# Attention: second score matmul over 128 rows instead of 64, rotary output split in place and stacked by copies

## The chip, the cores and the metric

One core of a Trainium2 chip runs the whole layer as one program. The metric is the device time of that program in microseconds (us); lower is better. The engines are TensorE (PE; its weight loads are shown apart as PEld), VectorE (DVE), ScalarE (ACT), GpSimd (POOL) and SyncE (SP), on whose queue all copies are issued here.

## What is computed

A decoder layer over 1024 tokens of width 1024: an mLSTM mixer and a differential attention in parallel, then cross attention, then a gated feed-forward part. The change lies in the differential attention, of 8 heads. Queries and keys of a head have two components `c` of 64 features, rotated by position; each component has its own causal softmax, and the second is subtracted with a factor:

```python
s = einsum('bhcqd,bhckd->bhcqk', qi, kt) * scale        # c = 0, 1; d = 64
s = where(kpos[None, :] <= qpos[:, None], s, -inf)
p = softmax(s, axis=-1)
a = p[:, :, 0] - lam * p[:, :, 1]
o = einsum('bhqk,bhkv->bhqv', a, vt)
```

Products are made nearly as exact as in float32: an operand is split into a high part (rounded to the type that PE takes fast, fp32r) and a low part, the rest; a product is the sum of high x high, high x low and low x high.

## The kernel before, in words

PE's order is written by hand. A queue of dense products (class `Weave`, L58) is issued in quanta, each of three or six matmuls, and the steps of the attention put their own matmuls between: `pump(n)` (L93) issues n quanta. The other engines' orders come from a list scheduler. All copies stand in one queue on SP, among them the loads of weights (`load_w`, L159), which the scheduler puts early.

For each head, `g_rope` (L606) makes queries (`which` 0) and keys (1): a dense product over 1024 features gives 128 rows, the two components of 64, by tokens, in two halves of 512 tokens. For each half, `ev` (L617) does: ACT reads the bank into `raw`; DVE shuffles it into `rot` and multiplies `raw` by a cosine; POOL multiplies `rot` by a sine; DVE adds. Then the result is split. Queries: tile `Q0` is to hold the high part of component 0 in rows 0 to 63 and its low part in rows 64 to 127, `Q1` the low part of component 1 above and its high part below. [...] Keys: `K0` holds the high part of component 0 twice, one above the other, `K1` that of component 1; a tile `klo` holds the low part of both components, 64 rows each.

So in `scores` (L664) one piece of scores takes two matmuls: L680 over 128 rows, (high + low of Q) x (high of K), and L681 over the 64 rows of one component, high of Q x low of K. In `Q1` and in `klo` component 1 lies in rows 64 to 127, so the second one uses rows 0 to 63 for component 0 and 64 to 127 for component 1. A block of 128 queries against n keys takes one or two such pieces per component; a head has 24, in groups `g` of two blocks, and after each piece one quantum of dense work. DVE reads each piece (L684, L687) for maximum and mask, ACT takes exp (L693), POOL scales the second component (L697), DVE combines (L698), and `values` (L702) transposes the weights on PE and multiplies by the values, a group later.

The buffers `raw`, `rot`, the values' `vt`, the gates' `gt` and the spills `ev` of the cross-attention products (L769) share a ring of `NROPE` buffers of 128x512. `Q`, `K` and `klo` have one buffer each, so the next head's halves wait for this head's last scores. Which dense products go into which head is set by `FILL` (L39); in head 7 these are products with 16 spills (`g_vo`) and the loads of the mLSTM's output (`g_load`).

Of the kernel before, what the change touches and what calls it, by code (L numbers as in the profile page):

```python
# [12 lines left out]
F = mybir.dt.float32  # L13
# [8 lines left out]
T = 1024  # L22
# [12 lines left out]
NROPE = 5  # L35
# [22 lines left out]
class Weave:  # L58
    """Order of the tensor engine's work: a queue of dense products, issued in quanta between
    the steps of the chains that wait for other engines, and steps that fall due after a  # L60
    number of quanta."""
# [54 lines left out]
def hybrid_layer(ctx: ExitStack, tc: tile.TileContext, a: dict, out: bass.AP):  # L116
# [74 lines left out]
    def g_fm(wsrc, acts, evac, pool=None, w=None):  # L191
        """128 features by the tokens of acts, K = 1024; evac(j, bank) per token half"""
# [10 lines left out]
    def g_tm(wsrc, nk, units, evac):  # L203
        """tokens by 256 features; units: (act pair, first token column); a bank holds two token tiles"""
# [41 lines left out]
    # ------------------------------------------- keys and values of the memory (cross attention)  # L246
# [42 lines left out]
    # ---------------------------------------------------------------- constants  # L289
# [42 lines left out]
    # ------------------------------------------------------------ mLSTM mixer  # L332
    with tc.tile_pool(name="ap", bufs=1, reuse_waits="tile") as A:
# [38 lines left out]
        def g_first():  # L372
            """values of head 0 and all input and forget gates: a bank per token tile"""
# [147 lines left out]
        # rotary tables  # L521
# [18 lines left out]
        # input and forget gates: partition = (head, chunk)  # L540
# [63 lines left out]
    # ------------------------------------------- differential attention mixer  # L604
    with tc.tile_pool(name="bp", bufs=1, reuse_waits="tile") as B:
        def g_rope(h, which):  # L606
            """rotary part of one head's queries or keys; stacked for two passes over 128 rows"""
            t_ = 16 + 8 * which + h
            if which == 0:
                dst = [B.tile([128, 1024], R, tag=f"Q{c}", name=f"Q{c}") for c in range(2)]  # L610
            else:
                dst = [B.tile([128, 1024], R, tag=f"K{c}", name=f"K{c}") for c in range(2)]
                klo = B.tile([128, 1024], R, tag="klo", name="klo")
                res["klo"] = klo
            res["Q" if which == 0 else "K"] = dst

            def ev(j, acc):  # L617
# [8 lines left out]
                to_hi(dst[0][:, js], raw, "g")  # L626
                to_hi(dst[1][:, js], raw, "s")
                if which == 0:
                    mv_ = B.tile([128, 512], R, tag="rhl", name="rlo", bufs=1)
                    to_lo(mv_, raw, dst[0][:, js], "v")  # L630
                    src = (mv_[0:64], mv_[64:128])
                else:
                    mv_ = B.tile([128, 512], R, tag="rhl", name="rhi", bufs=1)
                    to_hi(mv_, raw, "v")
                    to_lo(klo[:, js], raw, mv_, "v")
                    src = (mv_[0:64], mv_[64:128])
                dma(dst[0][64:128, js].bitcast(F), src[0].bitcast(F))
                dma(dst[1][0:64, js].bitcast(F), src[1].bitcast(F))
# [25 lines left out]
        def scores(h, g, qk):  # L664
            out_ = []
            for i in (2 * g, 2 * g + 1):
# [7 lines left out]
                for c in range(2):  # L674
                    run = None
                    for j, (c0, c1) in enumerate(cuts):
                        w = c1 - c0
                        sp = sm_tile("sp")
                        qs, cr = slice(i * 128, (i + 1) * 128), slice(c * 64, c * 64 + 64)
                        mm(sp[:, :w], qk[0][c][:, qs], qk[1][c][:, c0:c1], start=True)  # L680
                        mm(sp[:, :w], qk[0][c][cr, qs], qk[2][cr, c0:c1], stop=True)  # L681
# [91 lines left out]
        def g_qk(h):  # L773
            """Wq k^T of one head: [model dimension, memory keys]"""
# [12 lines left out]
        def g_vo(h):  # L787
            """v Wo of one head: [memory keys, model dimension]"""
# [175 lines left out]
    def pair(pool, tag, name, bufs):  # L964
        return (pool.tile([128, 8, 512], R, tag=tag, name=name + "h", bufs=bufs),
                pool.tile([128, 8, 512], R, tag=tag, name=name + "l", bufs=bufs))

    def g_add(wsrc, act, h, b, gb, dst=None):
        """z += act @ W for one half and 256 columns; the last block is followed by the norm"""
        def ev(u, acc):  # L970
            for i in range(2):
                ti = 4 * h + 2 * u + i
# [461 lines left out]
```

## Time and profile before

| what | us |
|---|---|
| median of three runs (lowest, highest) | 2325.5 (2322.64, 2325.77) |
| span of the profiled execution, first to last instruction | 2324.7 |
| PE busy in it | 2272.0 (98%), 14109 matmuls |
| DVE, ACT, POOL busy | 1437.7 (62%), 698.3 (30%), 730.1 (31%) |
| chain that ended last, share of PE | 85% |

Of the profiled execution no time but its span is shown; the median is 0.8 us above that span. The profile's page names the busy engine; what a stage waits for is read from the timeline of single engines (start, duration, instruction, and in brackets idle time before it with the releaser), and what a stretch holds from the table by windows. Starts of matmuls are measured; their ends are modelled, so durations of neighbours overlap.

### The profile page before, as it was taken

To read this page: it belongs to the slowest core of one execution; us is meant where nothing else is said; L and a number is where in the kernel's file an instruction comes from. 1 tells how busy PE (TensorE), PEld (TensorE's weight loads), DVE (VectorE), ACT (ScalarE), POOL (GpSimd) and SP (SyncE) were. 2 spreads that over 40 slices of the span, in tenths; PEclk is the share of its full clock that TensorE was granted. 3 is DMA by queue.
4 is the path that set the end of the run, shared out by engine and by line. 5 is a ranking of instruction groups with operands and counts; after the bars stand their busy time and mean duration, and the time that the engine had idled before them with its cause. 6 is when DMAs were issued, how large, how long until landed. Compare 5 with 4: busy or idle time off the path is not lost.

```text
span 2324.7 us, 36015 instructions
## 1 busy us (share of the span) xinstructions
PE 2272.0 (98%) x14109; PEld 2002.4 (86%) x14109; DVE 1437.7 (62%) x2671; ACT 698.3 (30%) x1375; POOL 730.1 (31%) x752
## 2 busy tenths in 40 slices
PE   8999999999999999999999999998899999999997
PEld 8898898877877877876888999998899999999996
DVE  8535644356677666667535477468866655566667
ACT  3322313234444444445332113313211111111122
POOL 7124413233243333334421223226411111211124
PEclk9999999999999999999999999999899999999999
DMA  8322212332142132126863423222211111111112
GB/s 315 113 62 86 100 46 100 121 108 71 42 135 77 42 109 65 49 68 196 278 214 136 175 89 101 82 91 64 64 47 46 55 55 55 46 46 55 55 57 98
DMA packets 87722, 221.68 MB, mean 95 GB/s; under 512 B 10080, under 2 KB 28416, under 8 KB 87552
## 3 DMA queue, kind: packets, MB, share of 16 engines
q1 hardware_dynamic: 87552, 219.37, 29.1%
q8 instruction: 111, 1.82, 0.3%
q14 instruction: 59, 0.48, 0.1%
HBM read 168.92 MB, written 41.98 MB: 91 GB/s over the span
## 4 chain that ended last, share of the span: by engine, by line
PE 85%; DVE 7%; POOL 2%; DMA 2%; issue 2%; ACT 1%; SPq 0%; DVEq 0%; POOLq 0%; ACTq 0%
PE acc L152 58%; PE xb L152 7%; PE xa L152 5%; PE xc L152 5%; PE sp L152 4%; PE op L152 2%; DVE wlo L149 1%; PE tp L727 1%; PE nm L152 1%; DVE d L1045 1%; DVE e L698 1%; PE kv L152 1%; ACT e L693 0%; DMA wraw<-oT_d 0%; DVE z L935 0%
## 5 line engine op out<-in xcount | busy, mean ns | idle before, releaser
L141 POOL TENSOR_SCALAR whi<-wraw 128x512 fp32r<-128x512 f32 (+1 forms) x250 | 181.7, 727 | 878.8 <-issue 355.4
L152 PE MATMUL acc<-bh,whi 128*128 128x512 f32 x1024 | 427.1, 417 | 0.9 <-DVE gt L849 0.5
L149 DVE TENSOR_TENSOR wlo<-wraw,whi 128x512 fp32r<-128x512 f32 (+1 forms) x379 | 307.6, 816 | 157.8 <-ACT whi L139 117.7
L152 PE MATMUL acc<-bh,wlo 128*128 128x512 f32 x1024 | 401.5, 392 | 0.0
L152 PE MATMUL acc<-bl,whi 128*128 128x512 f32 x1024 | 400.9, 392 | 0.0
L139 ACT ACTIVATE whi<-wraw 128x512 fp32r<-128x512 f32 (+1 forms) x252 | 157.6, 627 | 563.8 <-PE acc L152 284.2
L152 PEld LDWEIGHTS acc<-bh,whi 128*128 128x128 f32 x1024 | 192.8, 188 | 51.8 <-issue 15.7
L152 PEld LDWEIGHTS acc<-bh,wlo 128*128 128x128 f32 x1024 | 192.8, 188 | 42.1
L152 PEld LDWEIGHTS acc<-bl,whi 128*128 128x128 f32 x1024 | 193.3, 189 | 30.9
L152 PE MATMUL acc<-whi,bh 128*128 128x256 f32 (+1 forms) x728 | 218.5, 300 | 0.2 <-DVE ev L149 0.2
L152 PE MATMUL acc<-whi,bl 128*128 128x256 f32 (+1 forms) x728 | 205.5, 282 | 0.0
L152 PE MATMUL acc<-wlo,bh 128*128 128x256 f32 (+1 forms) x728 | 205.4, 282 | 0.0
L152 PE MATMUL xb<-xe,whi 128*128 128x256 f32 x1008 | 184.4, 283 | 11.0 <-DVE u L1045 8.1
L149 POOL TENSOR_TENSOR wlo<-wraw,whi 128x512 fp32r<-128x512 f32 (+1 forms) x125 | 174.0, 1392 | 9.8
L152 PEld LDWEIGHTS xb<-xe,whi 128*128 128x128 f32 x1008 | 156.4, 191 | 11.7 <-issue 7.2
L152 PEld LDWEIGHTS acc<-whi,bh 128*128 128x128 f32 x728 | 138.5, 190 | 11.2 <-issue 9.2
L152 PE MATMUL xb<-xe,wlo 128*128 128x256 f32 x504 | 143.0, 284 | 0.0
L152 PEld LDWEIGHTS acc<-wlo,bh 128*128 128x128 f32 x728 | 138.7, 191 | 0.8
L152 PEld LDWEIGHTS acc<-whi,bl 128*128 128x128 f32 x728 | 138.6, 190 | 0.0
L1255 DVE SCALAR_TENSOR_TENSOR z<-z,acc 128x512 f32<-128x512 f32 x144 | 98.2, 686 | 53.0 <-PE acc L152 51.6
L152 PE MATMUL xa<-xb,whi 128*128 128x256 f32 x672 | 125.1, 287 | 5.2 <-ACT u L1167 5.2
L152 PE MATMUL acc<-wlo,hidh 128*128 128x512 f32 x320 | 124.7, 390 | 1.4 <-DVE wlo L149 1.4
(320 smaller groups left out, 5257.9 us busy)
## 6 DMA issues: line engine op xcount, KB each, us to landing
wraw<-in_wfm_dram SPq DMA_DIRECT2D x48, 512.0 KB, 3.6
wraw<-in_wg_dram SPq DMA_DIRECT2D x24, 512.0 KB, 3.5
wraw<-in_wu_dram SPq DMA_DIRECT2D x24, 512.0 KB, 3.6
wraw<-in_wd_dram SPq DMA_DIRECT2D x22, 512.0 KB, 3.6
hT_d<-hp SPq DMA_DIRECT2D x16, 512.0 KB, 2.8
g_d<-gt SPq DMA_DIRECT2D x32, 256.0 KB, 2.2
gt<-g_d SPq DMA_DIRECT2D x16, 512.0 KB, 4.8
wraw<-in_wmix_dram SPq DMA_DIRECT2D x16, 512.0 KB, 4.2
```

Of the source, the lines that this page charges most:

```text
L139: S.activation(dst, src, AF.Copy)
L141: G.tensor_scalar(dst, src, 1.0, 0.0, op0=OP.mult, op1=OP.add)
L149: (V if eng == "v" else G).tensor_tensor(dst, src, hi.bitcast(F), op=OP.subtract)
L152: PE.matmul(o, l, r, start=start, stop=stop, skip_group_check=True)
L698: V.scalar_tensor_tensor(e[0][:, :n], e[0][:, :n], su[:, 0:1], e[1][:, :n], op0=OP.mult, op1=OP.add)
L727: PE.transpose(tp[:, kk * 256 + j * 128:kk * 256 + (j + 1) * 128], ab[j][:, kc], ident)
L1045: V.tensor_tensor(dst, x_, y_, op=op)
L1255: V.scalar_tensor_tensor(zs, zs, ALPHA if q == 0 else 1.0, acc, op0=OP.mult, op1=OP.add)
```

## The change

The high and the low part are now made in place: ACT writes the rounded high part of `raw` over `rot`, DVE the rest over `raw` (one subtraction). Everything else is done by copies of 64 rows x 512 tokens: four for a half of the queries (the high part of each component to its place, and the low part), eight for a half of the keys, of which the high part goes twice into `K0` or `K1` and the low part twice into `klo0` or `klo1`, one above the other. So the second matmul runs over 128 rows: (high + low of Q) x (low of K); the sum gains the term low x low. `klo` becomes two tiles, and the ring of shared buffers has four instead of five. The copies that POOL and ACT made of the high part, and DVE's copy `rhi`, are gone. Beside this the diff holds only comments and texts that were taken out.

```diff
@@ -35,1 +35,1 @@
-NROPE = 5
+NROPE = 4
@@ -601,18 +601,20 @@
                 W.pump(n)
         W.drain()
 
     with tc.tile_pool(name="bp", bufs=1, reuse_waits="tile") as B:
         def g_rope(h, which):
             t_ = 16 + 8 * which + h
+            dst = [B.tile([128, 1024], R, tag=f"{'QK'[which]}{c}", name=f"{'QK'[which]}{c}") for c in range(2)]
             if which == 0:
-                dst = [B.tile([128, 1024], R, tag=f"Q{c}", name=f"Q{c}") for c in range(2)]
+                res["Q"] = dst
+                to = [[(dst[0], 0), (dst[1], 64)], [(dst[0], 64), (dst[1], 0)]]
             else:
-                dst = [B.tile([128, 1024], R, tag=f"K{c}", name=f"K{c}") for c in range(2)]
-                klo = B.tile([128, 1024], R, tag="klo", name="klo")
-                res["klo"] = klo
-            res["Q" if which == 0 else "K"] = dst
+                klo = [B.tile([128, 1024], R, tag=f"klo{c}", name=f"klo{c}") for c in range(2)]
+                res["K"], res["klo"] = dst, klo
+                to = [[(kt, r) for kt in pr for r in (0, 64)] for pr in (dst, klo)]
 
             def ev(j, acc):
                 js = slice(j * 512, (j + 1) * 512)
@@ -623,19 +625,12 @@
                 V.tensor_tensor(raw, raw, cosT[:, js], op=OP.mult)
                 G.tensor_tensor(rot, rot, sinT[:, js], op=OP.mult)
                 V.tensor_tensor(raw, raw, rot, op=OP.add)
-                to_hi(dst[0][:, js], raw, "g")
-                to_hi(dst[1][:, js], raw, "s")
-                if which == 0:
-                    mv_ = B.tile([128, 512], R, tag="rhl", name="rlo", bufs=1)
-                    to_lo(mv_, raw, dst[0][:, js], "v")
-                    src = (mv_[0:64], mv_[64:128])
-                else:
-                    mv_ = B.tile([128, 512], R, tag="rhl", name="rhi", bufs=1)
-                    to_hi(mv_, raw, "v")
-                    to_lo(klo[:, js], raw, mv_, "v")
-                    src = (mv_[0:64], mv_[64:128])
-                dma(dst[0][64:128, js].bitcast(F), src[0].bitcast(F))
-                dma(dst[1][0:64, js].bitcast(F), src[1].bitcast(F))
+                to_hi(rot.bitcast(R), raw, "s")
+                V.tensor_tensor(raw.bitcast(R), raw, rot, op=OP.subtract)
+                for m, places in zip((rot, raw), to):
+                    for n, (t, r) in enumerate(places):
+                        c = n if which == 0 else n // 2
+                        dma(t[r:r + 64, js].bitcast(F), m[c * 64:c * 64 + 64])
             yield from g_fm(a["wfm"][t_], xT, ev)
 
         def g_vB(pr):
@@ -676,9 +671,9 @@
                     for j, (c0, c1) in enumerate(cuts):
                         w = c1 - c0
                         sp = sm_tile("sp")
-                        qs, cr = slice(i * 128, (i + 1) * 128), slice(c * 64, c * 64 + 64)
+                        qs = slice(i * 128, (i + 1) * 128)
                         mm(sp[:, :w], qk[0][c][:, qs], qk[1][c][:, c0:c1], start=True)
-                        mm(sp[:, :w], qk[0][c][cr, qs], qk[2][cr, c0:c1], stop=True)
+                        mm(sp[:, :w], qk[0][c][:, qs], qk[2][c][:, c0:c1], stop=True)
                         if j < len(cuts) - 1:
                             run = B.tile([128, 1], F, tag="run", name="run", bufs=2)
                             V.tensor_scalar(e[c][:, c0:c1], sp[:, :w], 1.0, None, op0=OP.mult, op1=OP.max,
```

What stands where is shown at three places. First PE, head 0, its first piece of scores for each component (`K_4362` and `K_4363` are K0 and K1 of that head): one piece of the difference.

```order
 L152 MATMUL acc<-bh,wlo 128x512
 L152 MATMUL sp<-K_4362,Q_4274 128x128
-L152 MATMUL sp<-klo,Q_4274 128x128
+L152 MATMUL sp<-klo_4364,Q_4274 128x128
 L152 MATMUL acc<-bh,whi 128x512
 L152 MATMUL acc<-bl,whi 128x512
 L152 MATMUL acc<-bh,wlo 128x512
 L152 MATMUL sp<-K_4363,Q_4275 128x128
-L152 MATMUL sp<-klo,Q_4275 128x128
+L152 MATMUL sp<-klo_4365,Q_4275 128x128
```

Only the tile of the second matmul differs, here and in all of PE's order; every matmul stands in the same place as before.

Second SP's queue where the keys of head 4 are made, of before (`rhi_7836` is the first half of 512 tokens, `rhi_7875` the second; `wraw` is a load of weights, `gt` a gate's spill):

```order
L638 DMA Q1_7604<-rlo_7777 64x512
L637 DMA K0_7781<-rhi_7836 64x512
L638 DMA K1_7782<-rhi_7836 64x512
L166 DMA wraw_8360<-in_wfm_dram 128x1024
L637 DMA K0_7781<-rhi_7875 64x512
L638 DMA K1_7782<-rhi_7875 64x512
L422 DMA g_d_76<-gt_7961 128x512
```

and with the change (`rot_7857` and `raw_7856` are the first half, `wraw_8395` is the same load of weights):

```order
L633 DMA Q1_7632<-raw_7796 64x512
L633 DMA K0_7809<-rot_7857 64x512 x2
L633 DMA K1_7810<-rot_7857 64x512 x2
L633 DMA klo0_7811<-raw_7856 64x512 x2
L633 DMA klo1_7812<-raw_7856 64x512 x2
L633 DMA K0_7809<-rot_7899 64x512 x2
L633 DMA K1_7810<-rot_7899 64x512 x2
L633 DMA klo0_7811<-raw_7898 64x512 x2
L633 DMA klo1_7812<-raw_7898 64x512 x2
L422 DMA g_d_76<-gt_7996 128x512
L166 DMA wraw_8395<-in_wfm_dram 128x1024
```

Eight copies stand where two stood, the low part's last, and the load of weights moves from between the halves to behind both and a spill.

Third POOL at the same place, before (`rot_7828` is the keys' first half):

```order
L754 TENSOR_TENSOR of_7760<-of_7760,rt_7807 128x256
L624 TENSOR_TENSOR rot_7828<-rot_7828,sinT_815 128x512
L141 TENSOR_SCALAR K0_7781<-raw_7827 128x512
L141 TENSOR_SCALAR whi_8051<-wraw_8045 128x512
L624 TENSOR_TENSOR rot_7867<-rot_7867,sinT_815 128x512
L141 TENSOR_SCALAR K0_7781<-raw_7866 128x512
L697 TENSOR_SCALAR e1_7904<-e1_7904,ssum_7906 128x128
```

and with the change:

```order
L749 TENSOR_TENSOR of_7788<-of_7788,rt_7836 128x256
L626 TENSOR_TENSOR rot_7857<-rot_7857,sinT_815 128x512
L141 TENSOR_SCALAR whi_8086<-wraw_8080 128x512
L626 TENSOR_TENSOR rot_7899<-rot_7899,sinT_815 128x512
L692 TENSOR_SCALAR e1_7939<-e1_7939,ssum_7941 128x128
```

POOL's copies of the high part are gone, the rest stands as before.

## Rows read from the trace of the kernel before

**Rows 1.** Table by windows: stretch, length, busy us (instructions) of each engine, clock, DMA share, GB/s.
```profile
497.60:1120.40 622.80, 613.10 (x3172) 474.33 (x3172) 424.36 (x1032) 279.34 (x598) 228.54 (x250) 0.99 0.31 94
```

**Rows 2.** Timeline of PE, head 1: start us, us, engine, line, instruction.
```profile
600.84 0.34 PE L152 MATMUL sp<-K,Q 128*128 128x384 f32 x1
601.11 0.43 PE L152 MATMUL sp<-klo,Q 64*128 64x384 f32 x1
601.48 0.39 PE L152 MATMUL acc<-whi,bh 128*128 128x256 f32 x1
601.70 0.28 PE L152 MATMUL acc<-wlo,bh 128*128 128x256 f32 x1
601.82 0.28 PE L152 MATMUL acc<-whi,bl 128*128 128x256 f32 x1
```

**Rows 3.** Timeline of PE's weight loads, same place; in brackets idle time before.
```profile
601.11 0.18 PEld L152 LDWEIGHTS sp<-klo,Q 64*128 64x128 f32 x1 [0.19 <-issue]
601.47 0.19 PEld L152 LDWEIGHTS acc<-whi,bh 128*128 128x128 f32 x1 [0.18 <-issue]
```

**Rows 4.** View of the tile klo: count, duration ns min/median/max, first and last start, forms.
```profile
L152 PE MATMUL sp<-klo,Q x192: 323/438/502, 497.8 to 1112.4; 64*128 64x384 f32 x80, 64*128 64x512 f32 x64, 64*128 64x256 f32 x32, 64*128 64x128 f32 x16
```

**Rows 5.** View of the tile raw, same columns: copies that the change takes out.
```profile
L143 DVE CAST rhi<-raw x16: 426/426/561, 483.0 to 1065.5; 128x512 fp32r<-128x512 f32 x16
L141 POOL TENSOR_SCALAR K<-raw x16: 622/852/862, 483.1 to 1065.6; 128x512 fp32r<-128x512 f32 x16
```

**Rows 6.** Timeline of SP, head 4: copies of the first half of the keys.
```profile
818.68 0.46 SPq L637 DMA_DIRECT2D K<-rhi  x1
819.25 0.54 SPq L638 DMA_DIRECT2D K<-rhi  x1
```

**Rows 7.** DMA issues from 497 to 1064: count, KB each, median us to landing.
```profile
K<-rhi SPq DMA_DIRECT2D x26, 128.0 KB, 2.2
```

**Rows 8.** Timeline of DVE: cast of the keys' first half, heads 2, 4, 5, 6.
```profile
652.50 0.43 DVE L143 CAST rhi<-raw 128x512 fp32r<-128x512 f32 x1
...
817.75 0.43 DVE L143 CAST rhi<-raw 128x512 fp32r<-128x512 f32 x1
...
896.96 0.43 DVE L143 CAST rhi<-raw 128x512 fp32r<-128x512 f32 x1
...
984.28 0.56 DVE L143 CAST rhi<-raw 128x512 fp32r<-128x512 f32 x1 [0.43 <-DMA Q<-rlo]
```

**Rows 9.** Timeline of PE: first klo matmul of heads 2, 4, 5, 6.
```profile
657.63 0.33 PE L152 MATMUL sp<-klo,Q 64*128 64x128 f32 x1
...
821.76 0.33 PE L152 MATMUL sp<-klo,Q 64*128 64x128 f32 x1
...
901.25 0.33 PE L152 MATMUL sp<-klo,Q 64*128 64x128 f32 x1
...
987.89 0.33 PE L152 MATMUL sp<-klo,Q 64*128 64x128 f32 x1
```

**Rows 10.** Windows: sum over 16 stretches, 8 pieces each, groups 2 and 3.
```profile
sum 178.60, PE 178.60 PEld 118.69 DVE 114.23 ACT 75.18 POOL 45.16; mean PE 11.16 PEld 7.42 DVE 7.14 ACT 4.70 POOL 2.82
```

**Rows 11.** Waits in the attention stage: us in total, times, longest us.
```profile
PE tp L727 <- DVE e L698: 8.6, 6, 2.2
...
DVE e L687 <- PE sp L152: 46.4, 64, 1.9
```

**Rows 12.** Windows: head 7, from its first score to the first product after.
```profile
1064.00:1120.40 56.40, 55.37 (x236) 37.86 (x235) 39.40 (x104) 33.40 (x72) 26.44 (x29) 1.00 0.92 294
```

**Rows 13.** DMA issues in head 7.
```profile
vo_d<-ev SPq DMA_DIRECT2D x14, 256.0 KB, 8.0
```

**Rows 14.** Windows: a stretch after PE's wait for softmax in head 0.
```profile
559.20:562.60 3.40, 3.40 (x12) 2.73 (x11) 2.57 (x6) 1.33 (x3) 0.62 (x1) 0.50 0.30 69
```

**Rows 15.** Timeline of SP, head 4: a load of weights.
```profile
820.84 0.33 SPq L166 DMA_DIRECT2D wraw<-in_wfm_dram  x1
```

**Rows 16.** Timeline of PE: the first product that uses these weights.
```profile
867.07 0.50 PE L152 MATMUL acc<-bh,whi 128*128 128x512 f32 x1
```

## The prediction

> **What bounds the kernel now.** I read the page first, to see which engine is busy nearly all the time and whose work makes up the chain that ended last: both are TensorE (PE). Then the table by windows, for the stage that the change touches, from the first score matmul at 497.6 us to the first product after the attention at 1120.4 us: 622.80 us, of which PE is busy 613.10, DVE 424.36, ACT 279.34 and POOL 228.54 [rows 1]. So time on PE is time. But a busy PE is not PE at its peak, so the next view is PE's timeline, where the reader is to look at the distance between *starts*, not at the durations. One dense 256-column product starts 0.12 us after another (601.70, 601.82). The pair that makes a piece of scores is slower: the 128-row matmul of K starts at 600.84, the 64-row matmul of klo at 601.11, the next dense product at 601.48 and the one after at 601.70 [rows 2]. That is 0.86 us from 600.84 to 601.70, for columns (384 + 384 + 256) that at 0.12 us per 256 would take 0.18 + 0.18 + 0.12 = 0.48 us. So **0.38 us** are lost at each pair: some 0.09 after the 128-row matmul, 0.19 after the 64-row one, 0.10 after the dense one behind it. PE's weight-load timeline says how: the load for the 64-row matmul begins only when that matmul itself begins, after 0.19 us in which the loader stood idle for nothing that the profile names, and the 128-row load after it again waits 0.18 us [rows 3]. Between matmuls that are all 128 rows high the loads lie under the matmul before, and the idle time is gone. There are 192 such pairs, in widths from 128 to 512 columns [rows 4].
>
> **The change part by part.**
>
> *Second score matmul over 128 rows.* The order of PE is the same row for row; only klo's height changes. If the cost hangs on the change of height, each pair loses its 0.38 us: 192 x 0.38 = **-73 us**, all on the path, since PE is what waits. I take the 384-column row for all widths (80 of the 192 have it); the 16 narrowest pairs may give less, as their weight loads set their pace. The matmul itself has the same columns, so the extra 64 rows cost nothing in this pace. A rule speaks against this term: the Trainium skill, "TensorE: Matmul & The Clock Gate", Part 3 (What overlaps and what doesn't), says that a weight load overlaps a running matmul only where the two use different row groups. By that rule the 128-row load of klo would wait as the 64-row one does, the term would be about 0 and the sum would come out as in the rival on height below. The rows disagree: loads of 0.19 us at matmuls that follow each other every 0.12 us, all on the same 128 rows [rows 2, 3], must overlap.
>
> *Copies on the engines.* POOL loses 16 copies of keys of 0.85 us and as many of queries, 27 us at most, DVE 16 casts of 0.43 us (7 us) [rows 5]; ACT's count stays. None of them is PE time, and POOL is busy for 37% of the stage. I cost it at nothing; if it helps, it is in the low end.
>
> *More DMA and a later arrival of keys.* A half (512 tokens) of a head's queries goes from two copies to four, of its keys from two to eight: over 8 heads of two halves, 64 become 192 issues on SP, each of 0.46 to 0.54 us and 0.57 us apart [rows 6], landing 2.2 us after issue [rows 7]. What can be late is the first half of the keys at a head's start. Now DVE's cast of K starts at 817.75 in head 4 [rows 8] and its first klo matmul at 821.76 [rows 9]. After the change the hi part is cast by ACT in about that place, 0.65 us; the first copy starts 0.5 us later (cast ends 818.18, copy starts 818.68 [rows 6, 8]), so 1.13 us after the point where the cast starts now. The first score needs both copies of klo0, the fifth and sixth in the queue: start 1.13 + 5 x 0.57 = 3.98, landing 2.2, so 6.2 us after that point. Head 4: 823.95 against 821.76, a wait of 2.2 us. The same for the other heads whose keys come late: head 2, 652.50 + 6.2 against 657.63, 1.1 us; head 5, 896.96 against 901.25, 1.9 us; head 6, 984.28 against 987.89, 2.5 us, less 0.4, since there the cast waited for a copy of the buffer that the change takes out [rows 8, 9]. Together **+7 us**. The second score, of the other component, comes after a dense step and waits for copies 2 x 0.57 us later; I cost it at nothing. Lower end 0 (POOL, freed of its copies, finishes the rotation sooner); upper end 16, where each landing takes twice the 2.2 us and four heads pay 2.2 us more.
>
> *Softmax behind a faster PE.* In the 16 stretches where eight pairs stand together (the scores of 512 to 1024 keys) DVE is busy 114.23 of 178.60 us [rows 10]. With 16 x 8 x 0.38 = 49 us less it would be 88% busy, on the path of exp, POOL's scaling and the transposes. PE now waits for that chain six times, 8.6 us in all [rows 11]. It is not overrun on average, but a piece of scores may be late. Bounds: 0, and one piece of 1.02 us (178.60 / 128 - 0.38) in each of the 16 stretches, 16 us; nearer the first, since it is DVE that now waits for scores (64 times, 46.4 us [rows 11]) and that has time to lose: **+5 us**.
>
> *Head 7.* From 1064 to 1120.4 the DMA engines are 92% busy at 294 GB/s [rows 12], and spills land after 8.0 us [rows 13]. The change cuts the buffers that spills, gates and rotary halves share from five to four. The 16 spills there need 4 rounds of some 8.5 us, 34 us, about the time that would be left for them. Head 7's share of the gain is 24 x 0.38 = 9.1 us; between none and all of it is lost: **+6 us**, nearer all than none because DMA has so little room.
>
> *Clock.* After one of the waits for softmax the granted clock was 0.50 for 3.4 us [rows 14], the lower of its two levels (1.2 GHz), which costs half of that, 1.7 us. Longer waits may bring one more such stretch: **+2 us**; bounds 0 and eight of them, 14 us.
>
> Sum: -73 + 7 + 5 + 6 + 2 = -53. The profiled span is 2324.7 us, so 2271.7; no time is shown for what lies around this span, and the median of the runs is 0.8 above it. I say **2272 us**.
>
> **The rivals.**
>
> *All of it is hidden.* POOL's 27 us make the rotation earlier, the chain keeps up, and the whole 73 us come through: 2252. For it: PE waits only 8.6 us in the stage now [rows 11]. Against: head 4's keys have no slack, and head 7's DMA none.
>
> *The chains become the pace.* All upper ends together would give -73 + 16 + 16 + 9 + 14 = -18, 2307; halfway from my sum to there, -35, stands for this case: 2290. For it: DVE at 88% [rows 10]. Against: DVE's 46.4 us of waiting for scores [rows 11].
>
> *Height is not the cause.* The loss belongs to the pair, whatever its rows: PE keeps its pace, the keys still come late, 2324.7 + 7 = 2332. By the rule of the Trainium skill above (same page and section) this is the case. Against: the dense products are 128 rows high, add into one bank as well, and keep 0.12 us [rows 2].
>
> *Weights come late (slower).* Weight loads stand in the same SP queue. In head 4 one is issued at 820.84, between the two halves of the keys, and used at 867.07 [rows 15, 16]; in the new order it stands behind the second half's eight copies and a gate's spill. If loads came 8 us too late in each of eight heads, PE would lose 64 us more: 2336. The point from which this makes the kernel slower is 53 / 8 = 6.6 us of waiting per head. Against: the margin there is 46 us, and the added issues of a head are 16 x 0.57 = 9 us.
>
> **How the numbers follow.** The forecast 0.65, all hidden 0.17, chains as the pace 0.12, height not the cause 0.03, weights late 0.03. The first three are all faster than by 0.2% (4.7 us, about what a measurement of this kernel can tell from no change); of the last two's 0.06 I give 0.02 to no change, for mixtures. Faster 0.94, same 0.02, slower 0.04. The range goes from just above the all-hidden case to the chain case: 2254 to 2294; the bounds of keys (0 to 16) and of head 7 lie inside it.
>
> **What would show it.** On PE's timeline the pair's two starts and the next one should be 0.17 to 0.18 us apart for 384 columns, with no idle time of the weight loader; the stage from first score to the first product after should take about 570 us. At heads 2, 4, 5 and 6 the first score should wait 1 to 2 us for a copy of klo. POOL and DVE lose 32 and 16 instructions. I am wrong if the 64-row gaps stay in the pairs, if ACT or SP are found waiting for the four shared buffers in every head, or if the transposes wait for DVE by more than some 15 us in all.

## The result, and the profile after

| | before | after |
|---|---|---|
| median, us (lowest to highest of 4 runs each) | 2324.18 (2322.64 to 2325.77) | 2286.71 (2285.06 to 2288.24) |
| span of the profiled execution, us | 2324.7 | 2283.3 |

The ratio is 0.9837, with a 95% interval of 0.9823 to 0.9851: faster, by 37.5 us of the medians and 41.4 us of the two profiled spans. The forecast was 2272, 53 us below the time before; the measured time lies in its range, 15 us above the forecast.

The page's first line shows what left the engines: no matmul, 32 instructions of POOL (720 for 752) and 16 of DVE (2655 for 2671).

```profile
PE 2207.3 (97%) x14109; PEld 2008.0 (88%) x14109; DVE 1421.2 (62%) x2655; ACT 696.4 (30%) x1375; POOL 704.9 (31%) x720
```

PE's timeline of the kernel after (start, duration, instruction; in brackets idle time before it and its releaser) at a pair of 384 columns in head 1, at the start of head 2, and in head 7:

```profile
600.42 0.34 PE L152 MATMUL sp<-K,Q 128*128 128x384 f32 x1
600.60 0.34 PE L152 MATMUL sp<-klo,Q 128*128 128x384 f32 x1
600.77 0.29 PE L152 MATMUL acc<-whi,bh 128*128 128x256 f32 x1
600.90 0.28 PE L152 MATMUL acc<-wlo,bh 128*128 128x256 f32 x1
...
641.30 0.22 PE L152 MATMUL sp<-K,Q 128*128 128x128 f32 x1
643.30 0.30 PE L152 MATMUL sp<-klo,Q 128*128 128x128 f32 x1 [1.77 <-DMA klo<-raw]
...
1061.67 0.40 PE L152 MATMUL sp<-klo,Q 128*128 128x512 f32 x1
1068.43 0.79 PE L152 MATMUL acc<-whi,kvh 128*128 128x512 f32 x1 [6.37 <-ACT ev L765]
```

The first four rows answer to [rows 2]: starts 0.18, 0.17 and 0.13 us apart, 0.48 in all where it was 0.86. The weight loader's (PEld's) timeline at the same pair answers to [rows 3]; there is no idle time in it, and the load for the 128-row klo begins at 600.43, while the matmul of K, on the same 128 rows, runs from 600.42:

```profile
600.30 0.19 PEld L152 LDWEIGHTS sp<-K,Q 128*128 128x128 f32 x1
600.43 0.19 PEld L152 LDWEIGHTS sp<-klo,Q 128*128 128x128 f32 x1
600.60 0.19 PEld L152 LDWEIGHTS acc<-whi,bh 128*128 128x128 f32 x1
```

The other four rows of PE's timeline are new: a wait for a copy of klo at a head's start, and one of 6.4 us in head 7. PE's waits over the attention (what waited, for what; us in total, times, longest) answer to [rows 11], where the transposes' 8.6 us for `e` stood:

```profile
PE tp L722 <- DVE e L693: 12.7, 7, 3.6
PE sp L152 <- DMA klo<-raw: 9.0, 7, 2.3
PE acc L152 <- ACT ev L765: 6.4, 1, 6.4
PE op L152 <- DVE atl L149: 3.7, 7, 1.6
PE acc L152 <- ACT whi L139: 1.0, 1, 1.0
```

The table by windows (window, its length, busy time and instructions of PE, PEld, DVE, ACT and POOL, granted clock, DMA share, GB/s) has the whole stage, from the first score to the mark at which [rows 1] end; then the seven stretches at half the clock, against [rows 14]; then five microseconds of head 7, against [rows 12]; last, of the kernel before, the only other stretch at half clock in its stage:

```profile
497.80:1082.20 584.40, 551.42 (x3172) 482.14 (x3171) 411.11 (x1018) 278.22 (x600) 205.71 (x222) 0.98 0.44 128
...
551.50:554.90 3.40, 2.71 (x8) 2.33 (x9) 3.12 (x5) 1.12 (x2) 0.90 (x1) 0.51 0.02 5
643.70:647.10 3.40, 3.40 (x18) 3.40 (x17) 3.29 (x9) 1.79 (x4) 1.41 (x1) 0.50 0.52 130
698.30:701.70 3.40, 3.08 (x9) 2.57 (x10) 3.09 (x6) 1.12 (x2) 0.53 (x1) 0.50 0.00 0
797.30:800.70 3.40, 3.07 (x9) 2.62 (x10) 1.14 (x7) 0.88 (x4) 0.00 (x0) 0.50 0.88 205
872.40:875.80 3.40, 3.40 (x10) 2.82 (x11) 1.60 (x10) 0.88 (x4) 0.23 (x1) 0.50 0.70 164
954.30:957.70 3.40, 3.40 (x11) 2.82 (x11) 1.14 (x7) 0.88 (x4) 0.37 (x1) 0.50 0.88 204
1066.90:1073.70 6.80, 5.27 (x12) 4.12 (x13) 1.96 (x4) 2.99 (x5) 0.62 (x1) 0.50 1.06 379
...
1060.00:1065.00 5.00, 2.06 (x11) 1.44 (x9) 2.16 (x9) 3.05 (x6) 2.71 (x4) 1.00 1.04 396
...
719.70:723.10 3.40, 3.40 (x13) 2.82 (x12) 1.95 (x4) 0.94 (x2) 0.14 (x1) 0.51 0.27 63
```

The stage is 584.4 us where it was 622.8, so 38.4 of the 41.4 us came from it. (The mark at its end is not the end of the attention: the last product of the values starts at 1135.3 before and at 1097.2 after. These are 38.1 us apart, so the reading stands.) The rows add up, nearly. *Pairs:* from the matmul of K to the second instruction behind it, 176 pairs take 0.38 to 0.40 us less, the 16 of 128 columns 0.28 (0.46 for 0.74): -73. *Waits:* 9.0 for klo, 12.7 + 3.7 - 8.6 = 7.8 for the softmax and its split, 6.4 + 1.0 = 7.4 in head 7: +24. *Clock:* PE was busy in 24.3 of 27.2 us at half clock, which costs, as an estimate, half of that, 12.2; in the kernel before, in all 6.8 us of two such stretches, 3.4 (the other is [rows 14]): +9. Together -40, against the measured -38.4. All seven stretches begin behind, or in, one of the eight waits of PE of more than 1.7 us; the eighth (2.64 us, for `e`, up to 1006.29) has none behind it. Five of the eight are new, the four for klo at heads 2, 4, 5 and 6 and the one for `ev`, and each of these five has a stretch. In the kernel before, two of three waits of 2.1 to 2.2 us have one.

Where the 6.4 us in head 7 come from is read on ACT's timeline: three spills stand still until one of the four buffers has been written out, while the DMA share is 1.04 to 1.06:

```profile
1067.78 1.86 ACT L765 ACTIVATE ev<-acc 128x512 f32<-128x512 f32 x3 [3.83 <-DMA vo_d<-ev]
```

### The profile page after: what moved, and what is told of

Its sections match the earlier page's. It is cut to its first block, busy times and chain, and to the rows that moved or that the text cites. A ratio compares the mean times of both kernels' runs of the same rounds, so it can differ in the third digit from the quotient of the medians.

```text
span 2283.3 us, 36224 instructions
## 1 busy us (share of the span) xinstructions
PE 2207.3 (97%) x14109; PEld 2008.0 (88%) x14109; DVE 1421.2 (62%) x2655; ACT 696.4 (30%) x1375; POOL 704.9 (31%) x720
## 4 chain that ended last, share of the span: by engine, by line
PE 51%; DVE 5%; DMA 2%; issue 2%; POOL 1%; ACT 1%; SPq 0%; DVEq 0%; POOLq 0%; ACTq 0%
PE acc L152 32%; PE xb L152 7%; PE xa L152 5%; PE xc L152 5%; DVE wlo L149 1%; DMA vo_d<-ev 1%; PE sp L152 1%; DVE d L1040 1%; PE op L152 1%; DVE z L930 0%; DVE xb L149 0%; PE tp L722 0%; DVE z L926 0%; DVE u L1040 0%; PE tp L1007 0%
## 5 line engine op out<-in xcount | busy, mean ns | idle before, releaser
L152 PE MATMUL acc<-bh,whi 128*128 128x512 f32 x1024 | 418.1, 408 | 0.4 <-ACT gtok L389 0.4
L152 PE MATMUL acc<-whi,bh 128*128 128x256 f32 (+1 forms) x728 | 213.2, 293 | 0.2 <-DVE ev L149 0.2
```

What stands on the lines that cost most here:

```text
L152: PE.matmul(o, l, r, start=start, stop=stop, skip_group_check=True)
```

## The experiments

Medians are of each kernel's runs; the kernel before was run beside each batch (medians 2324.36 to 2325.66), and the ratios are to that. A quantum is one step of the queue of dense products in `Weave`; filling work is what these quanta put between the steps of the attention; a seam is the place where one head ends and the next begins.

Where a few us decide, the end of the kernel is a poor place to look: behind the attention all these kernels have the same matmuls, and yet their profiled executions take 1152 to 1157 us there, with 21 to 34 us at half clock. So the time from the first score to one and the same place behind the attention (with 7850 matmuls left) is given as well, from the profiled execution: 671.7 us in the kernel before, 633.4 in the changed one.

**One line back.** The second matmul over 64 rows again, all else as changed:

```diff
-                        mm(sp[:, :w], qk[0][c][:, qs], qk[2][c][:, c0:c1], stop=True)
+                        mm(sp[:, :w], qk[0][c][cr, qs], qk[2][c][cr, c0:c1], stop=True)
```

> The changed kernel with one line back: the second score matmul runs over the 64 rows that hold the high part of the queries, as before the change; rotary output, copies and buffers stay as changed. Theory A (the change of height costs about 0.39 us in each of 192 pairs, and it alone is the gain): the pairs stand 0.86 us apart again in place of 0.47 (384 and 256 columns), +74 us, of which some 20 to 30 us are hidden again because the slower pace lets the key copies and the softmax catch up: 2330 to 2345 us, thus slower than the kernel before (2324). Theory B (the gain comes from fewer POOL and DVE instructions or from the copies, the height is incidental): 2283 to 2292 us, as the changed kernel, with pairs still 0.47 us apart.

Measured 2346.12 us (2337.70 to 2348.95), ratio 1.009 [1.0069, 1.0111]. PE's timeline of it, the pair that answers to [rows 2]:

```profile
600.24 0.34 PE L152 MATMUL sp<-K,Q 128*128 128x384 f32 x1
600.51 0.43 PE L152 MATMUL sp<-klo,Q 64*128 64x384 f32 x1
600.87 0.39 PE L152 MATMUL acc<-whi,bh 128*128 128x256 f32 x1
601.09 0.28 PE L152 MATMUL acc<-wlo,bh 128*128 128x256 f32 x1
```

The distance of 0.85 us is back, and each other width has its own of before. So the height is the gain, 59 us of it at the end of the kernel, and the rest of the change is a loss: without its matmul the kernel is 22 us slower than before. The profile is of the fastest execution, 13 us slower than before, and its waits account for that: PE waits 22.6 us in the stage where it waited 9.5, 8.0 of them for klo and 6.4 for `ev`, neither of which the kernel before has, and 10.2 us are at half clock for 6.8. The other three executions are 8 to 11 us longer, with a mean granted clock of 0.986 to 0.989 where this one has 0.993; no profile shows where. Theory A stands a little beyond its own upper end.

**The ring of shared buffers alone, on the kernel before** (`NROPE = 5` to `4`).

> The kernel before with the shared ring of rotary, value and spill buffers cut from 5 to 4, and nothing else. Theory A (the ring costs only in head 7, where the spills of v Wo wait for their copies out, and the slower pairs of the kernel before hide most of it): 2324 to 2330 us. Theory B (the smaller ring costs in every head, since the rotary output waits for the spills): 2330 to 2345 us. Theory C (head 7's wait in the changed kernel is due to full DMA queues, whatever the ring): 2322 to 2325 us.

Measured 2330.91 us (2325.67 to 2331.64), ratio 1.0028 [1.0015, 1.0040]: 6.6 us, at the edge of A and B. Its profile, taken in an execution of 2327.39 us, has 3.1 us of PE's waits for `ev`, both in head 7, a stretch of 6.8 us at half clock there, and no new wait in the other heads. Up to the same place it takes 4.1 us more than the kernel before. The ring costs in head 7, a few us, also with the slow pairs; what the longer executions have more is not shown.

**Order turned round in every second pair, on the kernel before.**

```diff
+                        odd = (c * len(cuts) + j) % 2 == 1
+                        if odd:
+                            mm(sp[:, :w], qk[0][c][cr, qs], qk[2][cr, c0:c1], start=True)
-                        mm(sp[:, :w], qk[0][c][:, qs], qk[1][c][:, c0:c1], start=True)
-                        mm(sp[:, :w], qk[0][c][cr, qs], qk[2][cr, c0:c1], stop=True)
+                        mm(sp[:, :w], qk[0][c][:, qs], qk[1][c][:, c0:c1], start=not odd, stop=odd)
+                        if not odd:
+                            mm(sp[:, :w], qk[0][c][cr, qs], qk[2][cr, c0:c1], stop=True)
```

> The kernel before, but every second pair issues its matmul of 64 rows first, so that two matmuls of 64 rows stand together and two of 128 rows stand together: 96 round trips between heights in place of 192, the same 192 matmuls of 64 rows. Theory A (the cost is in the change of height, 0.39 us a round trip): -37 us less what waits give back, 2287 to 2297 us. Theory B (the cost is in each matmul of 64 rows, or in each of its weight loads): 2322 to 2326 us. Theory C (also a step from rows 0 to 63 to rows 64 to 127 costs as much): where one chunk a tile is scored the two short matmuls are of different halves, 32 of the 96 saved round trips would stay: -25 us, 2299 to 2304 us.

Measured 2324.77 us, ratio 1.000 [0.9990, 1.0009], what B foresaw. But its timeline shows that the experiment did not do what its text says:

```profile
600.88 0.28 PE L152 MATMUL acc<-whi,bl 128*128 128x256 f32 x1
601.09 0.44 PE L152 MATMUL sp<-klo,Q 64*128 64x384 f32 x1
601.46 0.44 PE L152 MATMUL sp<-K,Q 128*128 128x384 f32 x1
601.74 0.28 PE L152 MATMUL acc<-whi,bh 128*128 128x256 f32 x1
```

Dense products stand between any two pairs, so each 64-row matmul still has 128-row ones on both sides, and the number of round trips is unchanged. It tells nothing between A and B. What it does show is that the cost hangs on place and not on operand: 0.21 into the short matmul, 0.37 out of it, 0.28 from the 384-column matmul behind it, which takes 0.18 among its like, the same sum as in [rows 2] though K and klo have changed places.

**Two pairs at a time, short matmuls next to each other, on the kernel before.**

```diff
+                    for sp, (c, (c0, c1)) in zip(sps, pairs):
+                        mm(sp[:, :c1 - c0], qk[0][c][:, qs], qk[1][c][:, c0:c1], start=True)
+                    for sp, (c, (c0, c1)) in zip(sps, pairs):
+                        cr = slice(c * 64, c * 64 + 64)
+                        mm(sp[:, :c1 - c0], qk[0][c][cr, qs], qk[2][cr, c0:c1], stop=True)
...
+                        yield 2 * PUMP_S
```

> The kernel before, but the scores are issued two pairs at a time: two matmuls of 128 rows, then two of 64 rows next to each other, then twice the filling products. The matmuls are the same 192 of 64 rows, the round trips between the heights fall from 192 to 96 (the run with the order turned round in every second pair left them at 192, since filling products of 128 rows stand between any two pairs). Theory A (the cost is in the change of height, 0.39 us a round trip): -37 us, of which waits may give back some 10: 2287 to 2300 us. Theory B (the cost is in each matmul of 64 rows or its weight load): 2322 to 2328 us. Theory C (a step from rows 0 to 63 to rows 64 to 127 costs as much as one from 128 to 64): 32 of the 96 are not saved, -25 us, 2299 to 2304 us.

Measured 2298.37 us (2298.12 to 2299.06), ratio 0.9887 [0.9872, 0.9902], 26 us faster with the same 192 matmuls of 64 rows. B is out. The number lies in A's range and only 0.6 us outside C's; the rows decide. First a block with two short matmuls of different halves (rows 0 to 63, then 64 to 127), then one with two of the same half, both of 512 columns:

```profile
503.21 0.61 PE L152 MATMUL sp<-K,Q 128*128 128x512 f32 x2
503.76 0.50 PE L152 MATMUL sp<-klo,Q 64*128 64x512 f32 x2
504.19 0.50 PE L152 MATMUL acc<-bh,whi 128*128 128x512 f32 x1
...
533.91 0.63 PE L152 MATMUL sp<-K,Q 128*128 128x512 f32 x2
534.47 0.73 PE L152 MATMUL sp<-klo,Q 64*128 64x512 f32 x2
535.13 0.50 PE L152 MATMUL acc<-bh,whi 128*128 128x512 f32 x1
```

From the first short matmul to the next dense product it is 0.66 us for two of the same half and 0.43 for two of different halves; one alone takes 0.42 to 0.43 in the kernel before. So a second one of the same half costs its columns (0.23) and nothing for a change; and one of the other half costs nothing at all (in all 32 such blocks its start is 3 to 4 ns behind that of the first). C has it the wrong way round. By these rows the edit saves 96 x 0.38 = 36 us and 32 second matmuls of 0.06 to 0.23, 5 us more; 13 us of new waits (22.4 for 9.5 us in PE's waits, 15.1 of them for `e`) leave 28, and 26 were measured. The Trainium skill, "TensorEngine Tiling (Array Packing)", Key Properties, says that changing the tiling mode drains TensorE, and that different tiles can work at the same time. Both agree with these rows: 0.38 us for going to 64 rows and back, and two halves in the time of one.

**Low part of the keys written in place beside rows of zeros.** No copies of klo; DVE writes 64 rows of each tile, the other 64 stay zero, and the second matmul keeps its 128 rows.

```diff
-                to = [[(kt, r) for kt in pr for r in (0, 64)] for pr in (dst, klo)]
+                to = [[(kt, r) for kt in dst for r in (0, 64)]]
...
+                    for c in range(2):
+                        cr = slice(c * 64, c * 64 + 64)
+                        V.tensor_tensor(res["klo"][c][cr, js], raw[cr], rot[cr], op=OP.subtract)
```

> The changed kernel, but the low part of the keys is not copied: it is written by two DVE subtractions of 64 rows each into two fixed tiles whose other 64 rows are zero throughout, so the second matmul still runs over 128 rows; the product of the two low parts is left out of the scores as in the kernel before. It has 64 copies fewer on SP's queue and 16 DVE subtractions more. Theory A (the late copies of the low part at heads 2, 4, 5 and 6 give back 9 us, and the half-clock stretches behind these four waits about 1.7 us each): 2269 to 2278 us, no wait for a copy at these heads, and at most 3 half-clock stretches in the stage in place of 7. Theory B (the copies' wait only stands in for a wait on DVE's softmax, which is the pace): 2282 to 2288 us, with the lost time at waits on e. Theory C (half-clock stretches come with the faster pace itself and not with the waits): 2276 to 2280 us, with 6 or 7 stretches left.

Measured 2282.57 us (2280.67 to 2285.20), ratio 0.9823 [0.9808, 0.9838]: 4.1 us below the changed kernel, in B's range. PE's waits in the stage:

```profile
PE tp L730 <- DVE e L701: 16.8, 11, 3.3
PE op L152 <- DVE atl L149: 6.9, 10, 1.6
PE acc L152 <- ACT ev L773: 3.0, 2, 2.4
```

The 9.0 us for klo are gone, as A said, and 3.4 of those for `ev`, but 7.3 are back at DVE's results (16.8 + 6.9 for 12.7 + 3.7), and six half-clock stretches are left where A allowed three. Six is what C foresaw, but each of them stands behind, or in, a wait of 1.4 to 3.3 us. Up to the same place the kernel takes 632.1 us, only 1.3 less than the changed one. Either the late copies had covered a late softmax, or the 16 subtractions that DVE has more, of 0.69 us each, make it late; no run tells these two apart.

**Spills of v Wo through the values' tags.**

```diff
-                    spill(acc, vo_d[2 * cb:2 * cb + 2, :, 2 * h + kt, :].rearrange("b p c -> p b c"))
+                    spill(acc, vo_d[2 * cb:2 * cb + 2, :, 2 * h + kt, :].rearrange("b p c -> p b c"),
+                          ("vh", "vl")[kt])
```

> The changed kernel, but the spills of v Wo in head 7 go through buffers of the values' tags, which stand empty there, and no longer through the ring of 4. Theory A (the ring of 4 is what makes the spill's ACT copy, and behind it TensorE, wait 6.5 us in head 7, with a half-clock stretch of 6.8 us behind it that costs half of that): 2277 to 2281 us, no wait on ev in head 7, at most 3.4 us at half clock there. Theory B (the DMA queues are full in head 7, so the wait only moves to the next transfer, a weight or a load of hT): 2284 to 2288 us, with a wait of 4 us or more on a DMA or on a weight in head 7.

Measured 2285.81 us, ratio 0.9828 [0.9812, 0.9845]: no difference from the changed kernel, and PE still waits 6.1 us for `ev`. It says nothing for B, though, since these tags have no more free buffers in head 7 (four, by the kernel's text) than the ring that they replace.

**Eight buffers for these spills**, the ring and the tags in turn: `(None, ("vh", "vl")[cb])[kt]` in place of the last line.

> The changed kernel, with the spills of v Wo in head 7 through the ring of 4 and four buffers of the values' tags in turn, so that eight can be on their way out (the run with the values' tags alone had only as many free buffers as the ring of 4, so it could not tell the ring from the transfers). Theory A (the DMA queues are full for some 25 us of head 7 and fall to about half afterwards, so more buffers let the spills wait while TensorE goes on): no wait on ev above 1 us, 2276 to 2281 us. Theory B (head 7 is bound by its transfers, and TensorE waits for a weight or for hT instead): 2284 to 2288 us, with a wait of 4 us or more on a DMA, a weight or hT.

Measured 2283.68 us (2277.62 to 2284.89), ratio 0.9814 [0.9794, 0.9834]; 3.0 us below the changed kernel, less than its own runs scatter; up to the same place it is 3.6 us ahead (629.8). PE's timeline in head 7:

```profile
1077.92 0.60 PE L722 MATMUL tp<-ident,e 128*128 128x128 f32 x4
1081.24 0.50 PE L152 MATMUL acc<-bh,whi 128*128 128x512 f32 x1 [2.72 <-DMA bh<-hT_d]
1082.56 0.67 PE L152 MATMUL acc<-bl,whi 128*128 128x512 f32 x1 [0.82 <-DMA bl<-hT_d]
```

There is no wait for `ev` left, and in its place 3.5 us for the loads of the mLSTM's output. Both theories have a part: PE waits 6.4 us with four buffers, and with eight the loads behind the same full DMA queues still make 3.5 (2.7 + 0.8).

**Four quanta ahead of the last values step of each head.** TensorE's order alone; the next head's fills are opened there.

```diff
+                for nm in FILL[h + 1] if h < 7 else ():
+                    add_fill(nm, h + 1)
+                W.pump(4)
                 yield from values(h, 3)
```

> The changed kernel, but four quanta of filling products (about 0.7 us each) are issued ahead of the last values step of every head instead of behind it; the list of fills of the next head is opened there. Same instructions on every engine, only TensorE's order differs. Theory A (what the faster pairs gave back lies at the seam of two heads: the last softmax of a head and the copies of the next keys are each waited for with nothing to fill the time, while 4 to 15 us of filling work stand right between the two): the waits on e (12.7 us) and on the copies of klo (9.0 us) mostly go, with the half-clock stretches behind them: 2262 to 2275 us. Theory B (DVE's chain of softmax instructions is the pace of the whole stage, so a wait that is filled at one place comes back at the next): 2282 to 2288 us, with as much waiting on DVE's results as before, at other places.

Measured 2282.08 us (2280.53 to 2283.73), ratio 0.9816 [0.9802, 0.9831]: 4.6 us below the changed kernel, at the lower edge of B; up to the same place it is 4.6 us ahead as well (628.8). PE's waits:

```profile
PE acc L152 <- ACT ev L765: 5.8, 2, 4.2
PE sp L152 <- DMA klo<-raw: 5.5, 5, 2.2
PE ss L152 <- POOL sqp L141: 4.6, 4, 1.7
PE op L152 <- DVE atl L149: 4.3, 9, 1.6
PE tp L722 <- DVE e L693: 2.4, 1, 2.4
```

The waits on `e` fell from 12.7 to 2.4 us, but 6.7 came up behind the sums of squares (4.6 here and 2.1 on `sqp` of DVE), which had been ready in time.

**The same and the values' tags for the spills together.**

> Both edits of this batch on the changed kernel: the four quanta ahead of the last values step, and the spills of v Wo in spare buffers. Theory A (the two losses are independent): the two gains add up, 2254 to 2268 us. Theory B (either the softmax chain or the DMA queues are the pace): 2278 to 2288 us.

Measured 2280.72 us (2279.86 to 2284.85), ratio 0.9814 [0.9799, 0.9829]: as without the tags, which was to be expected once these had turned out to add no buffer. A's sum failed.

**More of it: 8 quanta (16 in heads 3 and 5), `LAG_O` 8 for 5, and eight spill buffers.**

> The changed kernel with the eight spill buffers and more filling work at the seam of the heads: 8 quanta (16 in heads 3 and 5) ahead of the last values step, which is what the count of quanta shows to be left over there, and the sum of squares of an output is normed 8 quanta after it and not 5. Theory A (what the faster pairs gave back is a matter of where the filling products stand): no wait on the copies of klo at the heads' starts, waits above 0.55 us down from 33 to under 15 us in the stage, at most 14 us at half clock: 2262 to 2272 us. Theory B (DVE's chain is the pace): 2278 to 2284 us, waits of 25 us or more on e, atl or sqp at other places.

Measured 2283.56 us (2279.88 to 2284.82), ratio 0.9818 [0.9800, 0.9836]: B. PE's waits:

```profile
PE op L152 <- DVE atl L149: 11.3, 16, 1.7
PE ss L152 <- DVE sqp L149: 8.5, 7, 2.4
PE op L152 <- ACT ath L139: 5.3, 7, 1.1
```

No wait for klo, 0.2 us for `e`, and 10.2 us at half clock in the stage for 27.2: two of A's three marks. But PE's waits come to 33.7 us in all, as in the changed kernel (33.0): the fill that went to the seams is missing between the steps of the values, where 25 us of waits for `atl`, `ath` and `sqp` stand now. Filling work in the heads is limited; moved to one place, it leaves another.

**The three edits that each gained a little, together:** zero rows, four quanta, eight spill buffers.

> The three edits that each gained a little on the changed kernel, together: the low part of the keys written by DVE into tiles whose other rows are zero (no copies of it), four quanta of filling work ahead of the last values step, and eight spill buffers in head 7. Theory A (three independent losses: late copies, unfilled softmax at the seam, transfers in head 7): 4.1 + 4.6 + 3.0 us add up, 2270 to 2277 us. Theory B (DVE's chain of softmax and splits is the pace that all three run into, and the 16 subtractions more lengthen it): 2278 to 2284 us.

Measured 2275.28 us (2274.45 to 2278.69), ratio 0.9783 [0.9767, 0.9800]: 11.4 us below the changed kernel, the fastest of all, where the three single gains add up to 4.1 + 4.6 + 3.0 = 11.7. The interval of each single ratio overlaps that of the changed kernel, that of the three together does not. The profiles up to the same place (changed kernel, then this one) say the same without what happens behind:

```profile
497.80:1131.20 633.40, 600.42 (x3412) 523.43 (x3411) 438.42 (x1051) 293.27 (x624) 229.74 (x246) 0.98 0.46 136
...
497.30:1120.30 623.00, 597.63 (x3411) 517.54 (x3410) 452.65 (x1066) 290.13 (x623) 231.87 (x245) 0.99 0.41 126
```

These are 10.4 us, and the single edits give 1.3 + 4.6 + 3.6 = 9.5. So the three losses are separate, as A said, though each edit alone gives back part of what it takes.

**The same with half of the subtractions on POOL:** `(V, G)[c].tensor_tensor(...)`.

> The same, with the subtraction of the second half of each low part on POOL, so that DVE has as many instructions as in the changed kernel and POOL 16 more. Theory A (independent losses, DVE's load is not the limit): within 2 us of the run without it. Theory B (DVE's load is the limit): 3 to 6 us below it. Theory C (POOL's scaling of e stands in the same chain and gets 16 instructions ahead of it): 3 to 6 us above it.

Measured 2282.30 us (2280.50 to 2284.27), ratio 0.9815 [0.9800, 0.9829]: 7.0 us slower than with DVE alone, C, beyond its price; up to the same place it is 4.9 us (627.9), within it. The tile's groups (count, then shortest, median and longest in ns) give a reason:

```profile
L637 DVE TENSOR_TENSOR klo<-raw,rot x16: 682/684/1782, 482.4 to 1023.9; 64x512 fp32r<-64x512 f32 x16
L637 POOL TENSOR_TENSOR klo<-raw,rot x16: 1282/1794/2394, 482.5 to 1024.0; 64x512 fp32r<-64x512 f32 x16
```

POOL needs 1.79 us where DVE needs 0.68, and its scaling of `e` and its `sqp` stand behind that in the same queue: PE's waits on them rose from 5.5 to 9.5 us (`e`) and from 4.6 to 8.0 us (`sqp`), while those for DVE's `atl` and `sqp` fell from 9.8 to 5.6; and 17.1 us of the stage are at half clock for 10.2.

## Why the prediction was right or wrong

**The pairs: right.** -73 us was the term, the rows give -73, and the two runs on height (back to 64 rows: the distance of 0.85 us returns; half as many round trips: 26 us) show that the change of height is the cause. The rival "height is not the cause" is out, and with it, for matmuls of equal height in these traces, the rule of the Trainium skill, "TensorE: Matmul & The Clock Gate", Part 3 (What overlaps and what doesn't), by which a weight load waits for a matmul on the same row groups: the load at 600.43 lies under the matmul that started at 600.42.

**What is given back: the mechanisms were right, the sizes too small.** Forecast +20, found some +33 in the stage:

- *Clock*, +2: found +9. This is the term that was too small by most. The forecast counted "one more such stretch"; there were seven for two. The five new ones stand at the five new waits: the four at the heads' starts, which the forecast had listed, and the one in head 7, where it had expected a loss; it priced none of them with its stretch.
- *Softmax*, +5: found +7.8, in the order of the forecast; the transposes' 12.7 us stay below the 15 named as the mark of being wrong.
- *Keys*, +7: found 9.0, nearly all of it at the four heads named. (By its own terms, 0.65 and 0.5, the forecast's 1.13 us is 1.15; that moves no wait by more than 0.02.)
- *Head 7*, +6: found 7.4 of waits, for the reason given (DMA full, four buffers), and the longest half-clock stretch on top.
- *Copies taken from POOL and DVE*, 0: no run puts a gain on them.

Sum of the terms as found: -73 + 33 = -40, against -38.4 in the stage. All four losses lie inside the bounds that the forecast gave them, and all four above the value that it took, so the time is inside the range and above the forecast. The 3 us of the spans beyond the stage lie behind it, where the matmuls are the same: in the profiled execution PE waits 22.3 us there for 23.1, and one stretch of 3.4 us at half clock is missing, about 1.7 us. With the scatter of that part (1152 to 1157 us over these kernels) they are no gain of the change.

Of the three marks of being wrong none came: the gaps are gone from the pairs, the transposes wait 12.7 us, and outside head 7 ACT stands twice for copies out of the shared buffers (4.2 and 1.0 us), not in every head.

**The rivals.** "The chains become the pace" gave 2290, and the time is nearer to that than to the forecast. Its mechanism is half borne out. DVE's chain is not overrun (the fastest kernel has 16 subtractions more on DVE), but its results came late wherever a wait in front of them was taken out or filling work was moved away: 7.3 us more with the zero rows, 25 us behind the larger fills. "All hidden" (2252) is out. "Weights come late" did not occur: but for 1.2 us at split weights (1.0 for `whi`, 0.2 for `wlo`) PE waits for none in the stage. What was not foreseen is that the change without its matmul costs 22 us (13 in the profiled execution); the rival on height took 7.

**What stays open.** How much of head 7's loss belongs to the ring and how much to the queues is known only to within the scatter of the runs with four buffers (6 us between the lowest and the highest for the ring alone, 11 us for the one line back). Why some executions have more half-clock time behind the attention than others is not shown. The split of the kernel before, with its few copies and its five buffers, joined to the zero rows was not tried.

## What to carry to other kernels

Look at the distance between starts on TensorE wherever matmuls of different heights follow each other: each excursion to 64 rows among 128-row matmuls cost 0.38 us here (0.28 at 128 columns), which rows of zeros or a stacked operand avoid, and which short matmuls in a row share. When a term takes time off the bounding engine, list the waits that it will uncover, and count with a half-clock stretch behind each: in the changed kernel seven of the eight waits of more than 1.7 us had one. It is a risk and no rule: with the short matmuls next to each other one of four waits of 2.1 to 3.1 us had one, and with the zero rows two of 1.5 us did. A wait that is cured by moving filling work turns up where the work came from; here three edits added up, and two of them took something away (copies, a too small ring). And compare small edits over the stage that they touch, not only at the end of the kernel.

## What the runs showed of the hardware that was not expected

Two adjacent matmuls of 64 rows on different halves of the array took no longer than one: 0.43 us to the next product for two of 512 columns, against 0.66 on the same half and 0.42 to 0.43 for one alone. And the cost of a change of height is spread over three places whatever the operands are: 0.09 us ahead of the short matmul, 0.19 behind it, 0.10 behind the first 128-row matmul that follows.
